# Half-row transposes in pairs, and one double place in PSUM in place of two single ones, in a decoder step's sample attention

## The chip, the cores and the metric

The kernel runs on one core of one Trainium2 chip. The metric is the device time of one execution in microseconds; runs of one kernel are compared by their median. The profile and the trace come from one further, profiled execution. Engines are named as in the profile: PE is TensorE's matrix product, PEld its weight load, DVE is VectorE, ACT is ScalarE, POOL is GpSimd, SP is SyncE. L1513 is line 1513 of the kernel.

## The reference, cut to what matters

One inference step of a two-layer decoder: an mLSTM layer, then a forgetting-attention layer, each followed by a SwiGLU network. Two groups of requests share the weights: a prompt of 1024 tokens, and 8 sample requests of 8 new tokens each with 512 tokens of paged history. The change lies in the attention of the sample requests:

```python
kp = cache_k[page_table].reshape(Bd, n_pages * PAGE_SIZE, H_B, DH_B)     # 8 requests, 4 pages of 128 rows
...
s = jnp.einsum('bqhd,bkhd->bhqk', qi, k, preferred_element_type=f32)     # 16 heads of 64
s = s + ci.astype(f32).transpose(0, 2, 1)[..., None] - ckT[:, :, None, :]
s = jnp.where(pos_k[None, :] <= pi[:, None], s, -jnp.inf)
p = jax.nn.softmax(s, axis=-1)
return jnp.einsum('bhqk,bkhd->bqhd', p.astype(v.dtype), v)
```

## The kernel before

The stage that matters is `attend_sample`, called at the end of `phase_b`. It works request by request (b = 0 to 7) and, in a request, page by page (n = 0 to 3).

- `load(b)` issues the DMA of the request's keys, values and log-forget rows on SP's queue (request 0's small operands go through ScalarE's queue, L1478 to L1491). `kp` holds 4 pages of keys, 128 rows (positions) by 1024 columns (heads and dimensions).
- `turn(b, n)` transposes a page of keys with TensorE: eight transposes of 128 x 128 in 4-byte floats (L1513), each with the page's block as the loaded operand and the identity as the moving one. They go in two groups of four, each group into one PSUM bank (`ktp`, tag "kt"; the pool gives that tag two places of a bank each). VectorE copies the first group to `kT` in SBUF and ScalarE the second (L1514).
- `score(b, n)` multiplies queries with the transposed page, in tiles of 32 columns of the array (L1522). `new_keys(b)` does the same for the new tokens' keys (L1532), adds the forget terms and takes the row maximum on VectorE (L1535, L1537), and calls the exponentials on ScalarE (L1382).
- `turn_p(b)` transposes the request's weights, 128 rows by 576: four whole transposes into a place of tag "kt" (L1547), copied by ScalarE (L1548), and a fifth for the 64 new positions into a spare part of the bank of `new_keys` (L1549), copied by VectorE (L1550).
- `product(b)` multiplies the weights with the pages of values (L1559); `out(b)` transposes the result (L1570) and writes it to `ys`.

TensorE's order is written out by hand. Between these pieces stand calls f(n), each of which issues n times three matmuls of another work, the output gate of the layer: `gates()` in `phase_b` (L62 to L64, tile `bps`, 384 or 336 columns, whole rows of the array). Each gate tile of 24 matmuls ends with a sigmoid on ScalarE (L1328, tile `ogb`) that needs another activation table than the exponentials, so a table load stands between them. Where a weight of the gate is prepared, ScalarE rounds it (L126) and VectorE takes the remainder (L127). A round for the request x = b + 1 reads:

```python
load(x); f(2); turn(x, 0); f(2); turn(x, 1); f(2); turn_p(b); f(3)
score(x, 0); product(b); score(x, 1); f(2); turn(x, 2); f(2); out(b); turn(x, 3)
f(3); score(x, 2); score(x, 3); new_keys(x)
```

The order on the other engines is set by a scheduler when the kernel is built. A place of a tag is written again only after all readers of the tile that held it are done. The next stage, `attend_prompt`, loads its first operands on SP's queue (L1717). Elsewhere in the kernel stand other matmuls on half the array's rows, which the prediction reads: `scores` of the prompt attention (L1751), two heads on rows 0 to 63 and 64 to 127 into two banks, and `chunk_scores` of the mLSTM (L816); and small transposes of 16 rows in `forget` (L1368).

Of the kernel before, what the change touches and what calls it, by code (L numbers as in the profile page):

```python
# [7 lines left out]
F32 = mybir.dt.float32  # L8
# [8 lines left out]
P = 128  # L17
# [3 lines left out]
NS = NB * NQ  # L21
# [14 lines left out]
PAGE, NPG = 128, 4  # L36
PAST = PAGE * NPG
# [1431 lines left out]
def attend_sample(self, sk, sp, s2, pp, cq, ncn, masks, Y, fill):  # L1469


    nc, I, O = self.nc, self.I, self.O
# [3 lines left out]
    kt = sp.tile([P, 8, T0], F32, name="ktS")  # L1476
# [29 lines left out]
    def turn(b, n):  # L1506

        R = rows[b]
        kT = R["kT", n] = early.pop(0) if early else s2.tile([P, 8, PAGE], F32, name=f"kT{b}{n}", tag="kT")
        for g in range(2):  # L1510
            pk = pp.tile([P, 4, P], F32, name=f"ktp{b}{n}{g}", tag="kt")
            for j in range(4):
                nc.tensor.transpose(pk[:, j, :], R["kp"][n][:, (4 * g + j) * P : (4 * g + j + 1) * P], self.ident)  # L1513
            (nc.scalar.copy if g else nc.vector.tensor_copy)(kT[:, 4 * g : 4 * g + 4, :], pk)  # L1514

    def score(b, n):
        R = rows[b]
# [23 lines left out]
    def turn_p(b):  # L1541
        R = rows[b]
        s, pn = R["s"], R["pn"]
        pt = R["pt"] = s2.tile([P, 5, P], F32, name=f"ptS{b}", tag="ptS", bufs=1)
        ps = pp.tile([P, 4, P], F32, name=f"ptp{b}", tag="kt")
        for n in range(NPG):
            nc.tensor.transpose(ps[:, n, :], s[:, n * P : n * P + P], self.ident)  # L1547
        nc.scalar.copy(pt[:, :4, :], ps)  # L1548
        nc.tensor.transpose(pn[:NS, 64 : 64 + P], s[:, PAST:], self.ident)  # L1549
        nc.vector.tensor_copy(pt[:NS, 4, :], pn[:NS, 64 : 64 + P])  # L1550

    def product(b):
        R = rows[b]
# [23 lines left out]
    load(0)  # L1577
    f(3)
    turn(0, 0)
    f(2)  # L1580
    turn(0, 1)
    f(2)
    for n in range(NPG):
        score(0, n)
        f(2)
        if n + 2 < NPG:
            turn(0, n + 2)
            f(2)
    new_keys(0)
    for b in range(NB):  # L1590
        x = b + 1
        if x == NB:
            f(4)
            turn_p(b)
            f(3)
            product(b)
            f(3)
            out(b)
            break
        load(x)  # L1600
        f(2)
        turn(x, 0)
        f(2)
        turn(x, 1)
        f(2)
        turn_p(b)
        f(3)
        score(x, 0)
        product(b)
        score(x, 1)  # L1610
        f(2)
        turn(x, 2)
        f(2)
        out(b)
        turn(x, 3)
        f(3)
        score(x, 2)
        score(x, 3)
        new_keys(x)
# [3 lines left out]
    for g in range(2):  # L1623
# [9 lines left out]
        for j in range(4):  # L1633
            for z in range(2):
                r = slice(z * 64, z * 64 + 64)
                nc.vector.tensor_copy(Q[r, j, (2 * j + z) * NM : (2 * j + z + 1) * NM], qt[r, 4 * g + j, NS:])
        pn = pp.tile([P, 512], F32, name=f"mps{g}", tag="sn", bufs=1)
        for j in range(4):
            nc.tensor.matmul(pn[:, :NM], Q[:, j, :], kt[:, 4 * g + j, NS:], start=(j == 0), stop=(j == 3))
        s = s2.tile([P, NM], F32, name=f"sM{g}", tag="sM")  # L1640
# [6 lines left out]
        pt = s2.tile([NM, P], F32, name=f"ptM{g}", tag="ptM")  # L1647
# [6 lines left out]
        for z in range(2):  # L1654
            r = slice(z * 64, z * 64 + 64)
# [275 lines left out]
```

## Time and profile before

| | |
|---|---|
| three runs, median (lowest to highest) | 3142.53 us (3132.64 to 3145.92) |
| the profiled execution: its time, its span | 3134.74 us, 3133.0 us |
| PE busy; PEld busy | 3034.0 us (97%); 2883.1 us (92%) |
| DVE; ACT; POOL busy | 1265.6 us (40%); 950.2 us (30%); 412.2 us (13%) |
| granted TensorE clock, mean | 0.987 |
| sample attention, transposes at L1513 | 256, from 1716.6 us to 1861.9 us of the span |

Times in the profile are microseconds from the span's start, and means of one instruction are in nanoseconds. A row of the timeline gives start, length, engine, line, operation, output and inputs, the loaded operand's rows x columns and the moving one's shape, and in brackets the engine's idle time before it with what ended it. Matmuls are pipelined, so that the length of one is more than the distance to the next.

### The profile page before, as it was taken

Reading aid. Unit: us, or ns where it says so; the run is one execution under the profiler, and the core shown is the slowest. Engines: PE = TensorE matmul, PEld = TensorE weight load, DVE = VectorE, ACT = ScalarE, POOL = GpSimd, SP = SyncE. Lnnn points to the kernel's source line nnn. Section 1 sums busy time; section 2 is a strip of 40 time slices with the busy share of each in tenths; the row PEclk is TensorE's granted clock in tenths of the full one; section 3 lists DMA queues with packets and bytes.
Section 4 is the critical chain, followed back from the end, with each engine's and each line's share of the span. In section 5 each row is a group of like instructions: output and inputs, shape, how many; then the busy total and the mean of one; then the engine's idle time right before and its main releaser. Section 6 shows DMA issues by size and latency. Waiting matters only on the chain.

```text
span 3133.0 us, 50924 instructions
## 1 busy us (share of the span) xinstructions
PE 3034.0 (97%) x21182; PEld 2883.1 (92%) x21182; DVE 1265.6 (40%) x2678; ACT 950.2 (30%) x1873; POOL 412.2 (13%) x806
## 2 busy tenths in 40 slices
PE   7999989999999999999999998999999999999998
PEld 7998879999999999999999886777999999999998
DVE  5132545633333333272455433554453333333323
ACT  5122453311111111142445445666331111111112
POOL 2011322100000000044453011222210000000002
PEclk9999999999999999999999998999999999999999
DMA  6142544111111111134444854332311111111111
GB/s 212 33 117 82 140 120 123 47 48 41 45 43 41 48 41 48 41 112 141 152 156 126 297 207 167 110 124 75 113 48 41 47 41 43 45 41 48 41 41 58
DMA packets 243314, 277.85 MB, mean 89 GB/s; under 512 B 26510, under 2 KB 193866, under 8 KB 243082
## 3 DMA queue, kind: packets, MB, share of 16 engines
q1 hardware_dynamic: 215426, 195.88, 19.9%
q0 software_dynamic: 23984, 76.40, 7.5%
q8 instruction: 166, 2.72, 0.4%
q10 hardware_dynamic: 3672, 2.31, 0.3%
q14 instruction: 66, 0.54, 0.1%
HBM read 211.35 MB, written 63.18 MB: 88 GB/s over the span
## 4 chain that ended last, share of the span: by engine, by line
PE 79%; DVE 4%; ACT 2%; DMA 2%; issue 1%; POOL 0%; SPq 0%; ACTq 0%; DVEq 0%; POOLq 0%
PE fps L63 11%; PE fps L62 11%; PE fps L64 11%; PE dps L62 5%; PE dps L63 5%; PE dps L64 5%; PE tmps L62 3%; PE tmps L63 3%; PE tmps L64 3%; PE sp L1751 3%; PE tp L1793 2%; PE op L1816 2%; PE pops L64 2%; PE pops L63 2%; PE pops L62 2%
## 5 line engine op out<-in xcount | busy, mean ns | idle before, releaser
L133 DVE TENSOR_TENSOR slot<-slot,slot 128x1024 fp32r<-128x1024 f32 x140 | 171.9, 1229 | 483.7 <-ACT slot L132 483.6
L132 ACT CAST slot<-slot 128x1024 fp32r<-128x1024 f32 x140 | 147.1, 1051 | 707.9 <-PE dps L63 393.7
L62 PE MATMUL dps<-ah,slot 128*128 128x384 f32 (+1 forms) x1056 | 353.1, 334 | 6.1 <-DVE vA L1075 3.1
L63 PE MATMUL dps<-al,slot 128*128 128x384 f32 (+1 forms) x1056 | 349.1, 331 | 0.0
L64 PE MATMUL dps<-ah,slot 128*128 128x384 f32 (+1 forms) x1056 | 348.7, 330 | 0.0
L205 POOL TENSOR_TENSOR ns<-ns,nq 128x384 f32<-128x384 f32 (+1 forms) x72 | 80.9, 1123 | 1717.6 <-ACT nq L203 1717.5
L62 PE MATMUL fps<-x1h,slot 128*128 128x384 f32 x704 | 236.9, 337 | 0.0
L62 PE MATMUL fps<-x2h,slot 128*128 128x384 f32 x704 | 236.5, 336 | 0.0
L63 PE MATMUL fps<-x2l,slot 128*128 128x384 f32 x704 | 236.5, 336 | 0.0
L64 PE MATMUL fps<-x2h,slot 128*128 128x384 f32 x704 | 236.5, 336 | 0.0
L64 PE MATMUL fps<-x1h,slot 128*128 128x384 f32 x704 | 236.5, 336 | 0.0
L63 PE MATMUL fps<-x1l,slot 128*128 128x384 f32 x704 | 236.4, 336 | 0.0
L64 PE MATMUL fps<-x0h,slot 128*128 128x336 f32 x704 | 223.0, 317 | 0.0
L62 PE MATMUL fps<-x0h,slot 128*128 128x336 f32 x704 | 222.5, 316 | 0.0
L63 PE MATMUL fps<-x0l,slot 128*128 128x336 f32 x704 | 222.4, 316 | 0.0
L62 PEld LDWEIGHTS dps<-ah,slot 128*128 128x128 f32 x1056 | 198.3, 188 | 13.9 <-DVE vA L1075 6.6
L63 PEld LDWEIGHTS dps<-al,slot 128*128 128x128 f32 x1056 | 198.5, 188 | 0.2
L64 PEld LDWEIGHTS dps<-ah,slot 128*128 128x128 f32 x1056 | 198.3, 188 | 0.0
L1053 DVE TENSOR_TENSOR fs<-fps,fs 128x336 f32<-128x336 f32 x132 | 71.4, 541 | 282.7 <-PE fps L64 282.7
L1075 DVE TENSOR_TENSOR Ht<-Ht,dps 128x384 f32<-128x384 f32 (+1 forms) x240 | 125.7, 536 | 106.0 <-PE dps L64 106.0
L1075 DVE TENSOR_TENSOR vA<-vA,dps 128x384 f32<-128x384 f32 (+1 forms) x240 | 125.4, 535 | 91.2 <-PE dps L64 91.2
L132 ACT CAST ah<-fs 128x336 fp32r<-128x336 f32 x132 | 65.7, 498 | 282.0 <-DVE fs L1053 282.0
(560 smaller groups left out, 7335.2 us busy)
## 6 DMA issues: line engine op xcount, KB each, us to landing
slot<-in_w_gate_up SPq DMA_DIRECT2D x88, 512.0 KB
slot<-in_w_down SPq DMA_DIRECT2D x44, 512.0 KB
kp<-in_cache_k SPq DMA_DIRECT2D x32, 512.0 KB
vp<-in_cache_v SPq DMA_DIRECT2D x32, 512.0 KB
wraw<-in_w_in_a SPq DMA_DIRECT2D x24, 512.0 KB
ncb<-cD SPq DMA_DIRECT2D x16, 520.0 KB
slot<-in_w_qo_b SPq DMA_DIRECT2D x16, 512.0 KB
slot<-in_w_kvf SPq DMA_DIRECT2D x14, 512.0 KB
```

The lines of the kernel that those rows point to most:

```text
L62: mm(ps, sh, mh, start=first, stop=False)
L63: mm(ps, sh, ml, start=False, stop=False)
L64: mm(ps, sl, mh, start=False, stop=last)
L132: self.nc.scalar.copy(hi, src)
L133: self.nc.vector.tensor_tensor(out=lo, in0=src, in1=hi.bitcast(F32), op=ALU.subtract)
L205: (nc.vector if x == KT - 1 else nc.gpsimd).tensor_tensor(out=s, in0=s, in1=sq, op=ALU.add)
L1053: nc.vector.tensor_tensor(out=s[:, :n], in0=ps[:, :n], in1=s[:, :n], op=ALU.mult)
L1075: nc.vector.tensor_tensor(out=H[t][:, m], in0=H[t][:, m], in1=o, op=ALU.add)
L1751: nc.tensor.matmul(ps[z][:, :n], a[r, qs], b[r, at : at + n], start=(x == 0), stop=(x == 2 and not diag))
L1793: nc.tensor.transpose(pt[:, x, z, u * P : u * P + P], ss[z, u][:, (j0 + x) * P : (j0 + x + 1) * P], self.ident)
L1816: mm(po[ds[z], :256], vr[:, j0 + x, ds[z]], th[:, x, z], start=(j0 + x == 0), stop=False)
```

## The change

In `turn`, a page's block of 128 columns is transposed in two halves, rows 0 to 63 and rows 64 to 127 of the page, each with its part of the identity. All sixteen halves of a page go into one tile of two banks, the first halves into one and the second into the other, the two halves of a block one behind the other in the order. VectorE copies the bank of the first halves, ScalarE that of the second. In `turn_p` the weights are transposed likewise, the new positions with them in the same tile. The tile has the tag "kt" with one place of two banks in place of two places of one bank. In the built program TensorE issues 16 transposes a page in place of 8 and 10 per request for the weights in place of 5. The scheduler's order for ScalarE, VectorE and SP differs from before inside this stage alone; GpSimd's is the same.

```diff
         kT = R["kT", n] = early.pop(0) if early else s2.tile([P, 8, PAGE], F32, name=f"kT{b}{n}", tag="kT")
-        for g in range(2):
-            pk = pp.tile([P, 4, P], F32, name=f"ktp{b}{n}{g}", tag="kt")
-            for j in range(4):
-                nc.tensor.transpose(pk[:, j, :], R["kp"][n][:, (4 * g + j) * P : (4 * g + j + 1) * P], self.ident)
-            (nc.scalar.copy if g else nc.vector.tensor_copy)(kT[:, 4 * g : 4 * g + 4, :], pk)
+        pk = pp.tile([P, 2, 8, 64], F32, name=f"ktp{b}{n}", tag="kt", bufs=1)
+        for j in range(8):
+            for h in range(2):
+                r = slice(h * 64, h * 64 + 64)
+                nc.tensor.transpose(pk[:, h, j], R["kp"][n][r, j * P : j * P + P], self.ident[r, r])
+        for h in range(2):
+            (nc.scalar.copy if h else nc.vector.tensor_copy)(kT[:, :, h * 64 : h * 64 + 64], pk[:, h])
...
         pt = R["pt"] = s2.tile([P, 5, P], F32, name=f"ptS{b}", tag="ptS", bufs=1)
-        ps = pp.tile([P, 4, P], F32, name=f"ptp{b}", tag="kt")
-        for n in range(NPG):
-            nc.tensor.transpose(ps[:, n, :], s[:, n * P : n * P + P], self.ident)
-        nc.scalar.copy(pt[:, :4, :], ps)
-        nc.tensor.transpose(pn[:NS, 64 : 64 + P], s[:, PAST:], self.ident)
-        nc.vector.tensor_copy(pt[:NS, 4, :], pn[:NS, 64 : 64 + P])
+        ps = pp.tile([P, 2, 8, 64], F32, name=f"ptp{b}", tag="kt", bufs=1)
+        for n in range(NPG + 1):
+            m = P if n < NPG else NS
+            for h in range(2):
+                r = slice(h * 64, h * 64 + 64)
+                nc.tensor.transpose(ps[:m, h, n], s[r, n * P : n * P + m], self.ident[r, r])
+        half = lambda x: x.rearrange("p n (h q) -> p h n q", h=2)
+        nc.scalar.copy(half(pt[:, :4]), ps[:, :, :4])
+        nc.vector.tensor_copy(half(pt[:NS, 4:5]), ps[:NS, :, 4:5])
```

## The prediction

> **What bounds the kernel now.** I read the page first, for the engine that carries the chain, then the stage in which the edited lines run, by windows, and inside it the timeline.
>
> ```profile
> span 3133.0 us, 50924 instructions
> ...
> PE 3034.0 (97%) x21182; PEld 2883.1 (92%) x21182; DVE 1265.6 (40%) x2678; ACT 950.2 (30%) x1873; POOL 412.2 (13%) x806
> ...
> PE 79%; DVE 4%; ACT 2%; DMA 2%; issue 1%; POOL 0%; SPq 0%; ACTq 0%; DVEq 0%; POOLq 0%
> ...
> 1716.00:1742.00 26.00, 19.80 (x154) 16.41 (x156) 8.91 (x32) 8.96 (x17) 4.31 (x8) 0.80 0.96 320
> ...
> 1742.00:1868.00 126.00, 124.77 (x1477) 107.95 (x1477) 51.71 (x159) 58.76 (x103) 7.59 (x14) 1.00 0.71 255
> ...
> L1513 PE MATMUL ktp<-ident,kp 128*128 128x128 f32 x256 | 35.2, 279 | 5.4 <-DVE kT L1514 2.7 <-DVE blo L1272 1.4 <-ACT kT L1514 1.2
> ```
>
> TensorE bounds the kernel. The windows show the stage of the sample attention: first 26 us in which TensorE has holes and its clock is at 0.80, then 126 us in which it is busy for 124.77 and everything added to its queue is added to the end. The last row is what the change replaces: 256 whole transposes, eight for each of 32 pages. Nothing after this stage hides a delay: the loads of the next stage wait for one of this stage's last matmuls.
>
> ```profile
> SPq L1717 <- PE pom L1652: 5.4, 1, 5.4
> ```
>
> Now one round of the stage (a request's new pages 0 and 1, then the weights of the request before), out of the timeline with other rows left out. Columns: start in us, length, engine, line, operation.
>
> ```profile
> 1778.56 0.34 PE L64 MATMUL bps<-x1h,slot 128*128 128x384 f32 x1
> ...
> 1778.73 1.03 PE L1513 MATMUL ktp<-ident,kp 128*128 128x128 f32 x8
> ...
> 1779.14 0.78 ACT L1382 ACTIVATE sS<-sS,nb 128x576 f32<-128x576 f32 x1 [2.33 <-DVE nb L1380]
> ...
> 1779.44 0.69 DVE L1514 COPY kT<-ktp 128x512 f32<-128x512 f32 x1 [0.33 <-PE ktp L1513]
> ...
> 1779.78 0.34 PE L63 MATMUL bps<-x1l,slot 128*128 128x384 f32 x1
> ...
> 1779.91 0.57 ACT L1514 COPY kT<-ktp 128x512 f32<-128x512 f32 x1
> ...
> 1779.95 0.34 PE L64 MATMUL bps<-x1h,slot 128*128 128x384 f32 x1
> ...
> 1780.65 1.04 PE L1513 MATMUL ktp<-ident,kp 128*128 128x128 f32 x8
> ...
> 1781.78 0.59 ACT L1514 COPY kT<-ktp 128x512 f32<-128x512 f32 x1 [1.30 <-PE ktp L1513]
> ...
> 1781.88 0.34 PE L64 MATMUL bps<-x1h,slot 128*128 128x384 f32 x1
> ...
> 1782.38 1.28 ACT L1328 ACT_TABLE_LOAD   x1
> ...
> 1782.39 0.34 PE L64 MATMUL bps<-x2h,slot 128*128 128x384 f32 x1
> ...
> 1782.57 0.60 PE L1547 MATMUL ptp<-ident,sS 128*128 128x128 f32 x4
> ...
> 1783.29 0.34 PE L63 MATMUL bps<-x2l,slot 128*128 128x384 f32 x1
> ...
> 1783.68 0.49 ACT L1328 ACTIVATE ogb<-bps 128x384 f32<-128x384 f32 x1
> ...
> 1784.07 0.58 ACT L1548 COPY ptS<-ptp 128x512 f32<-128x512 f32 x1
> ```
>
> The reader is to see that TensorE never stops here, that a gate matmul follows the next at 0.17 (1779.78 to 1779.95), and that the weights' transposes at 1782.57 run while ScalarE is still at the page's second copy (until 1782.37) and has the table load and the gate's sigmoid (ogb) still before it. Before the change they needed only VectorE's place of the pair, which was free.
>
> **What the transposes cost, before and after.** Before, a page takes from L64 at 1778.56 to the second gate matmul at 1779.78, 1.22, less two gate periods of 0.17: 0.88. The weights take 1783.29 - 1782.39 - 0.34 = 0.56. So a whole transpose is 0.11.
>
> Half-row transposes in pairs are not in this trace. Half-row matmuls in pairs are, and so are transposes with few moving columns:
>
> ```profile
> 1909.58 0.34 PE L64 MATMUL og<-x1h,wlo 128*128 128x384 f32 x1
> ...
> 1909.85 0.79 PE L1751 MATMUL sp<-k,q 64*128 64x384 f32 x6
> ...
> 1910.85 0.34 PE L63 MATMUL og<-x1l,whi 128*128 128x384 f32 x1
> ...
> 326.89 1.16 PE L816 MATMUL sps<-qk 64*128 64x128 f32 x16
> ...
> 1457.17 0.66 PE L1368 MATMUL fgcq<-ident,cnB 16*128 16x16 f32 x8 [1.10 <-DVE cnB L1364]
> ...
> L1368 PE MATMUL fgcq<-ident,cnB 16*128 16x16 f32 x8 | 0.7, 210 | 1.1 <-DVE cnB L1364 1.1
> ```
>
> The first three rows price the way into half rows and out again: 1910.85 - 1909.58 = 1.27, less two gate periods and three pairs of the same 0.17 each, leaves 0.41 that whole rows do not pay. L816 shows that two halves run side by side in plain 4-byte data too: 16 passes of 128 columns in 1.16, where one after the other at 0.11 would take 1.76. L1368 gives the beat of transposes that load 128 columns and move few: (0.66 - 0.21) / 7 = 0.064. With 64 moving columns the moving side needs half of 0.11, 0.055, so the load's 0.064 is the later of the two; I take 0.064 for a pair (0.055 to 0.11, the upper end if the two halves take turns). In the 0.41 is a first load that nothing hides; at L1368's beat it should be some 0.05 shorter than in the L1751 rows (an estimate), so I take 0.36 for the way in and out, with 0.41 as the upper end and nothing as the lower (transposes with fewer rows might not pay it).
>
> A page: 0.36 + 8 x 0.064 = 0.87 against 0.88. The weights, five pairs: 0.36 + 0.32 = 0.68 against 0.56. So the 32 pages gain 0.3 together and the eight weights lose 1.0. What halving the rows saves goes into entering and leaving.
>
> The copies move as many elements and I cost them as before (0.69, 0.57). Both now start behind the last pair, VectorE's about 0.1 later and ScalarE's earlier than before. The small loads nm and cm, which the change moves ahead of some of request 1's pages on SP's queue, are short, and no row of TensorE waits for a page; I cost them at nothing (a page that came late would cost its lateness once).
>
> **One place in place of two.** Now a block may begin only when both copies of the block before are done. In the built program the queue of ScalarE for a round reads: exponentials, copy of page 0, table load, sigmoid ogb, copy of page 1, copy of the weights; before, page 1's copy stood ahead of the table load. And ogb waits for a gate matmul that TensorE issues behind page 1's transposes. The round above, by its own rows: page 0 starts at 1778.83 (0.10 of way in, as 1909.85 - 1909.58 - 0.17), its last pair at 1779.34; 0.21 for that pair (L1368's mean) and 0.09 to the copy (1781.69 to 1781.78) make the copies ready at 1779.64, VectorE's done at 1780.33; ScalarE's stays at 1779.91 to 1780.48, because the exponentials of 1779.14 hold it. Six gate matmuls later page 1 would start at 1780.72: no wait. Its last pair starts at 1781.23, the last gate matmul of ogb at 1781.83 and ends at 1782.17. ogb then starts at 1782.20; the copy follows 0.39 behind it (as 1784.07 follows 1783.68), 1782.59 to 1783.18; the weights' transposes start at 1783.23. Unwaited they would start at 1782.62. Behind TensorE's waiting instruction stand nine gate matmuls, the scores and the products, all on the path. The stall is 0.61, and the round's third block ends 0.69 later than before. Pages 2 and 3 have no sigmoid between their copies. So five such rounds: 5 x 0.67 = 3.4.
>
> Two of the seven rounds are worse, since a late exponential holds page 0's copy:
>
> ```profile
> 1763.27 0.56 ACT L1514 COPY kT<-ktp 128x512 f32<-128x512 f32 x1
> 1763.74 0.70 ACT L126 ACTIVATE slot<-slot,gain 128x128 fp32r<-128x128 f32 x2
> ...
> 1763.89 0.66 PE L1513 MATMUL ktp<-ident,kp 128*128 128x128 f32 x4 [0.61 <-ACT kT L1514]
> ...
> 1765.38 0.60 PE L1547 MATMUL ptp<-ident,sS 128*128 128x128 f32 x4
> ```
>
> Here half of page 1 was already done when TensorE waited. After, all of it starts at 1763.89, and on ScalarE one rounding of a weight (0.4, two take 0.70), the table load, ogb and the copy follow: 1763.8 + 0.4 + 1.28 + 0.39 + 0.58, so the weights start near 1766.45, not 1765.38. With the way out of their block 1.1 each (the second such round begins near 1813.5), 2.2.
>
> The start of the stage:
>
> ```profile
> 1722.46 0.66 PE L1513 MATMUL ktp<-ident,kp 128*128 128x128 f32 x4 [1.92 <-DVE kT L1514]
> ...
> 1726.09 0.52 PE L63 MATMUL bps<-x1l,slot 128*128 128x384 f32 x1
> 1726.41 0.52 PE L64 MATMUL bps<-x1h,slot 128*128 128x384 f32 x1
> ...
> 1726.74 0.60 ACTq L1491 DMA_DIRECT2D nck<-csE  x1
> ...
> 1727.38 1.07 ACT L1514 COPY kT<-ktp 128x512 f32<-128x512 f32 x2 [6.22 <-DMA qDh<-bhi]
> ...
> 1728.49 1.11 DVE L1503 COPY qb<-qtS 64x32 f32<-64x32 f32 x8 [4.65 <-DMA qtS<-qS]
> ...
> 1729.00 1.08 PE L1522 MATMUL sps<-kT,qb 128*32 128x128 f32 x16 [2.07 <-DVE qb L1503]
> ```
>
> ScalarE's first copy sits behind its own loads until 1727.38. Before, page 1 and six gate matmuls were done meanwhile and TensorE then idled 2.07 for qb. After, page 1 starts at about 1728.0; page (0.87 to 1.5) and gates (6 x 0.17, or 6 x 0.32 at the low clock of the 1726.09 rows) put the first scores at 1729.9 to 1731.4, not 1729.0: 0.9 to 2.4, I take 1.7 since the clock is low there.
>
> Sum: 3.4 + 2.2 + 1.7 + 0.1 (the last weights; request 0's other pages come out even) = +7.4 us. The profiled execution lasted 3134.7 (its span 3133.0 and 1.7 around it) and would become 3142.1. The median of the three runs, 3142.5, lies 7.8 above that execution; the same addition gives 3149.9.
>
> **Rivals.**
> - The waits do not bind, only the ways in and out: the sum keeps the blocks' 0.7 and 1.7 of the start, 3145. For it: the stall hangs on ogb's place in one queue. Against: the built order has it in all seven rounds. Chance 0.18.
> - The pairs take turns. This is the way to slower: two half-row transposes, moved and loaded one after the other, 0.064 more per pair, (32 x 8 + 8 x 5) x 0.064 = 19 on top of 7.4, 3169. It decides from a beat of about 0.09 for a pair. Against it stands L816; for it, that no row has two transposes at once. Chance 0.09.
> - The loads set a slower beat. If a half-row load of 128 columns takes as long as a whole transpose does, 0.11 instead of 0.064, 296 pairs add 13.6: 3163.5. L1368's beat speaks against it, though its loads have 16 rows. Chance 0.08. (The Trainium skill, TensorE: Matmul & The Clock Gate, section LDWEIGHTS, has this rule: a load lasts its columns divided by 1.2 ns, whatever its rows, which is 107 ns for 128; by it halving rows would save nothing. L1368's 64 ns disagrees with it.)
> - The promise holds: no price for entering half rows and no new wait. A page falls from 0.88 to 0.57, 32 x 0.31 + 8 x 0.18 = 11.4 less, 3131. Against: every half-row block in the trace pays. Chance 0.05.
>
> **How the numbers follow.** The forecast of 3149.9 has 0.60. About 0.5% (15.7 us) is what a measurement of this kernel can tell from no change; its three runs lie 13.3 apart. Slower by more: the two slow-beat rivals, 0.17, and a little of the forecast's own upper edge, 0.19 in all. Faster by more: only the promise with luck in the runs, 0.02. The range leaves out the promise and the turn-taking pairs: from 3136 (the first rival, with runs as far below as those of before lie) to 3164 (the slow loads).
>
> **What would show it.** In the trace of after: a beat of 0.055 to 0.07 in 16 half-row transposes and a page at 0.87; TensorE's idle time before ptp, put down to the ScalarE copy, near 0.6 in five rounds and more in two; about 7.5 us of idle in front of the second page of request 0, and scores starting 1 to 2.4 later; the stage's end 7 later; the rest unchanged. It would be wrong with a beat near 0.11, with ptp unwaited, or with a page well under 0.8.

## The result: 3151.9 us, 0.35% longer

| | before | after |
|---|---|---|
| median (lowest to highest), eight runs each | 3141.36 us (3132.64 to 3146.31) | 3151.91 us (3145.08 to 3158.26) |
| ratio, 95% interval | | 1.0035 (1.0018 to 1.0052) |
| profiled execution: time, span | 3134.74, 3133.0 us | 3153.29, 3151.6 us |
| the stage, in the profiled execution | 150.7 us | 166.9 us |

The forecast of 3149.9 is 2 us off and inside its range; the time stays within the 0.5% that the prediction took for no change. That hides that the sum behind it was too small where it can be checked. **The stage** is measured here, and for every kernel below, from the last gate matmul ahead of the first page's transposes to the last request's weights' transposes: 1716.63 to 1867.28 before, 1719.00 to 1885.89 after. It grew by 16.2, and the prediction's terms gave 7.4. Behind that point both executions are alike (1265.7 us to the end in each), ahead of it they differ by 2.4, as executions of one kernel do.

The page and the windows of the changed kernel:

```profile
span 3151.6 us, 51506 instructions
...
PE 3040.3 (96%) x21478; PEld 2877.6 (91%) x21478; DVE 1267.4 (40%) x2678; ACT 950.2 (30%) x1873; POOL 412.2 (13%) x806
...
PE 79%; DVE 4%; ACT 3%; DMA 2%; issue 2%; POOL 0%; ACTq 0%; SPq 0%; DVEq 0%; POOLq 0%
```

```profile
1716.00:1742.00 26.00, 17.17 (x172) 13.97 (x170) 10.59 (x38) 9.02 (x21) 4.16 (x8) 0.87 0.93 300
1742.00:1868.00 126.00, 113.59 (x1530) 88.83 (x1530) 47.51 (x147) 53.64 (x95) 7.05 (x13) 0.97 0.69 251
```

In the same 126 us TensorE was busy for 124.77 before and is for 113.59 now: the work is no longer the limit, it waits. The groups of TensorE in the stage (busy, mean of one in ns, then the idle time ahead of them and what ended it) say where:

```profile
L1514 PE MATMUL ktp<-ident,kp 64*128 64x64 f32 x512 | 23.5, 234 | 15.4 <-ACT kT L1516 10.3 <-DMA kp<-in_cache_k 2.9 <-DVE blo L1272 1.7
...
L1552 PE MATMUL ptp<-ident,sS 64*128 64x64 f32 x64 | 3.7, 235 | 6.8 <-ACT kT L1516 6.8
```

That is 22.2 of idle time, against 5.4 ahead of the pages' transposes and the 2.07 for qb before: 14.7 more. ScalarE's copy of a page ends 17.1 of the 22.2 (1.2 before). The round that answers to the one shown of before (same request, other rows left out):

```profile
1790.06 0.34 PE L64 MATMUL bps<-x1h,slot 128*128 128x384 f32 x1
...
1790.33 0.71 PE L1514 MATMUL ktp<-ident,kp 64*128 64x64 f32 x16
...
1791.15 0.69 DVE L1516 COPY kT<-ktp 128x512 f32<-128x512 f32 x1 [0.54 <-PE ktp L1514]
1791.25 0.34 PE L63 MATMUL bps<-x1l,slot 128*128 128x384 f32 x1
...
1791.88 0.59 ACT L1516 COPY kT<-ktp 128x512 f32<-128x512 f32 x1 [0.37 <-DVE kT L1516]
1791.95 0.34 PE L64 MATMUL bps<-x1h,slot 128*128 128x384 f32 x1
1792.48 1.28 ACT L1328 ACT_TABLE_LOAD   x1
...
1792.52 0.71 PE L1514 MATMUL ktp<-ident,kp 64*128 64x64 f32 x16 [0.23 <-ACT kT L1516]
...
1793.27 0.69 DVE L1516 COPY kT<-ktp 128x512 f32<-128x512 f32 x1 [1.36 <-PE ktp L1514]
...
1793.98 0.49 ACT L1328 ACTIVATE ogb<-bps 128x384 f32<-128x384 f32 x1 [0.21 <-PE bps L64]
...
1794.13 0.34 PE L64 MATMUL bps<-x2h,slot 128*128 128x384 f32 x1
1794.37 0.58 ACT L1516 COPY kT<-ktp 128x512 f32<-128x512 f32 x1
...
1795.00 0.52 PE L1552 MATMUL ptp<-ident,sS 64*128 64x64 f32 x10 [0.53 <-ACT kT L1516]
```

The reader is to see three things. The block itself is as forecast: 1791.25 - 1790.06 less two gate periods is 0.85, and 0.71 less the mean length of one, 0.23, leaves 0.48 for fifteen steps, 0.032 for a transpose or 0.064 for a pair. The wait behind the sigmoid is as forecast: the weights start at 1795.00, 0.87 behind the gate matmul at 1794.13, where an unwaited block starts 0.27 behind (1790.33 after 1790.06). And one thing was not forecast: ScalarE's copy of page 0 at 1791.88 waits for VectorE's copy of the same page, 1791.15 to 1791.84, and so page 1 has to wait too. Before the change both copies ran together (1779.44 and 1779.91). The list of waits in the stage (us in total, times, the longest) has this as the largest wait of ScalarE; it is idle time of ScalarE, of which only a part reaches TensorE:

```profile
ACT kT L1516 <- DVE kT L1516: 60.9, 18, 8.5
...
PE ktp L1514 <- DMA kp<-in_cache_k: 2.9, 1, 2.9
```

### The profile page after: what moved, and what is told of

It is laid out like the page before. It is cut to its first block, busy times and chain, and to the rows that moved or that the text cites. A ratio compares the mean times of both kernels' runs of the same rounds, so it can differ in the third digit from the quotient of the medians.

```text
span 3151.6 us, 51506 instructions
## 1 busy us (share of the span) xinstructions
PE 3040.3 (96%) x21478; PEld 2877.6 (91%) x21478; DVE 1267.4 (40%) x2678; ACT 950.2 (30%) x1873; POOL 412.2 (13%) x806
## 3 DMA queue, kind: packets, MB, share of 16 engines
q1 hardware_dynamic: 215426, 195.88, 19.9%
## 4 chain that ended last, share of the span: by engine, by line
PE 79%; DVE 4%; ACT 3%; DMA 2%; issue 2%; POOL 0%; ACTq 0%; SPq 0%; DVEq 0%; POOLq 0%
PE fps L63 11%; PE fps L62 11%; PE fps L64 11%; PE dps L62 5%; PE dps L63 5%; PE dps L64 5%; PE tmps L62 3%; PE tmps L63 3%; PE tmps L64 3%; PE sp L1756 3%; PE tp L1798 2%; PE op L1821 2%; PE pops L64 2%; PE pops L63 2%; PE pops L62 2%
```

## Experiments

First a table of the stages; "ratio" is to the kernel before, run on the same chip in the same job.

| kernel | stage, us | ratio (95% interval) |
|---|---|---|
| before | 150.7 | 1 |
| after | 166.9 | 1.0035 (1.0018 to 1.0052) |
| e1, halves of kT unbroken | 165.5 | 1.0044 (1.0027 to 1.0061) |
| e2, whole rows in one place | 169.9 | 1.0083 (1.0064 to 1.0101) |
| e3, half rows, two places | 154.3 | 1.0012 (0.9999 to 1.0026) |
| e4, halves not in pairs | 174.8 | 1.0067 (1.0045 to 1.0089) |
| e5, a tile for each half | 153.1 | 1.0021 (1.0004 to 1.0037) |
| e6, no sigmoid | 160.9 | 1.0046 (1.0031 to 1.0061) |
| e7, four loads for 32 | 169.3 | 1.0050 (1.0031 to 1.0069) |
| e8, two pages at a time; again | 144.0; 143.6 | 0.9987 (0.9970 to 1.0003); 0.9996 (0.9981 to 1.0010) |
| e9, e8 with the small loads | 146.3 | 1.0006 (0.9993 to 1.0019) |

The stage is the sharper measure, since it leaves out what executions of one kernel differ by elsewhere; it comes from one execution each.

**Why the copies follow one another.** The first guess was the interleaved destinations: VectorE's half and ScalarE's half of kT lie in alternating runs of 64.

```diff
-kT = ... s2.tile([P, 8, PAGE], F32, ...)
+kT = ... s2.tile([P, 2, 8, 64], F32, ...)
-    (nc.scalar.copy if h else nc.vector.tensor_copy)(kT[:, :, h * 64 : h * 64 + 64], pk[:, h])
+    (nc.scalar.copy if h else nc.vector.tensor_copy)(kT[:, h], pk[:, h])
```

> The changed kernel, but kT is laid out by halves (half, eight parts, 64 keys), so that each of a page's two copies writes one unbroken half of its tile; the scores read it across the two halves; nothing else differs (every engine's queue has the same order). The stage is measured from the last gate matmul before the first page's transposes to the last request's weights' transposes: 150.7 us before, 166.9 after. Theory 1 (the two copies of a page follow one another in the changed kernel because their destinations interleave in one tile): ScalarE's copy starts beside VectorE's again, the waits before pages 1 and 3 (0.2 to 0.4 each, 14 of them) go, the waits of the weights behind the sigmoid stay near 0.6: the stage lasts 162 to 163. Theory 2 (they follow one another because they read one PSUM tile): no change, 166 to 168.

```profile
ACT kT L1516 <- DVE kT L1516: 60.8, 18, 8.0
```

Theory 1 fell: the wait is the same (60.8 against 60.9), so are the waits before pages 1 and 3, and the stage is 165.5, a little below the range that theory 2 gave. The destination is not what orders the copies.

**One place without half rows.**

```diff
-for g in range(2):
-    pk = pp.tile([P, 4, P], F32, name=f"ktp{b}{n}{g}", tag="kt")
-    for j in range(4):
-        nc.tensor.transpose(pk[:, j, :], R["kp"][n][:, (4 * g + j) * P : (4 * g + j + 1) * P], self.ident)
-    (nc.scalar.copy if g else nc.vector.tensor_copy)(kT[:, 4 * g : 4 * g + 4, :], pk)
+pk = pp.tile([P, 8, P], F32, name=f"ktp{b}{n}", tag="kt", bufs=1)
+for j in range(8):
+    nc.tensor.transpose(pk[:, j, :], R["kp"][n][:, j * P : (j + 1) * P], self.ident)
+for g in range(2):
+    (nc.scalar.copy if g else nc.vector.tensor_copy)(kT[:, 4 * g : 4 * g + 4, :], pk[:, 4 * g : 4 * g + 4, :])
```

> The kernel before with its whole-row transposes, but a page's eight and a request's four of the weights go into one place of two banks with one buffer, as in the change: one place without half rows. Theory 1 (the loss is the one place and what it does to the order on ScalarE): the weights wait near 0.6 in five rounds and about 2 in two, the second page of request 0 waits for ScalarE's first copy, no waits before page 3, and one page of request 2 may come late (up to 3) as in the changed kernel, since SyncE's order is nearly that of the changed kernel: the stage lasts 159 to 162. Rival (the loss is the half rows, in and out of their mode): 151 to 153.

```profile
ACT kT L1514 <- DVE kT L1514: 64.5, 18, 8.2
...
PE ktp L1512 <- ACT kT L1514: 13.9, 15, 7.3
...
PE ptp L1547 <- ACT kT L1514: 6.8, 7, 2.1
```

The rival (half rows cost) fell. But 169.9 is above what theory 1 gave too, since the copies follow one another here as well, with unbroken destinations and whole rows. And with one place whole rows are the worse choice: by the rows of one round in each kernel their eight transposes take 1.03 - 0.28 = 0.75 from the first to the last, not 0.48, and the first copy can begin only then; in five rounds TensorE waits 0.6 to 0.7 before page 1 (0.3 to 0.4 in the changed kernel), and in all seven 0.5 to 0.6 before page 3 (0.2 to 0.3).

**Half rows with two places, and half rows with one place but a tile for each half.** Both give each half its own tile of one bank. e3 leaves the pool two places and the weights whole rows in VectorE's place; e5 has one place per half, for pages and weights, as the change has.

```diff
-pk = pp.tile([P, 2, 8, 64], F32, name=f"ktp{b}{n}", tag="kt", bufs=1)
+pk = [pp.tile([P, 8, 64], F32, name=f"ktp{b}{n}{h}", tag="kt") for h in range(2)]                    # e3
+pk = [pp.tile([P, 8, 64], F32, name=f"ktp{b}{n}{h}", tag=f"kt{h}", bufs=1) for h in range(2)]        # e5
...
+ps = [pp.tile([P, 8, 64], F32, name=f"ptp{b}{h}", tag=f"kt{h}", bufs=1) for h in range(2)]           # e5
```

> The changed kernel's half rows in pairs for the pages alone, each half in a bank of its own with two places as before, kT by halves, and the weights by whole rows into VectorE's place as before: half rows without one place. Theory 1: a page block of 0.85, no wait of the weights behind the sigmoid, ScalarE's order as before; the second page of request 0 still waits for ScalarE's first copy (about 1.5), and a page of request 2 may come late (up to 3), since SyncE's order is that of the changed kernel; the pages gain 32 x 0.035 = 1.1: the stage lasts 151 without a late page, 154 with one. Rival (half rows are what costs): over 158.

> The changed kernel, but each half has a tile and a one-bank place of its own (one buffer each) in place of one two-bank tile, for the pages and for the weights; the destinations interleave as in the change. So there is still only one place per half, but no instruction shares a tile with the other half's copy. In the built program ScalarE's copy of page 1 then stands ahead of the table load and the sigmoid, as in the kernel before. Theory A (the one tile is the cause: ScalarE's copy waits for VectorE's, and the scheduler, which plans with that wait, puts page 1's copy behind the sigmoid): copies side by side, no wait before pages 1 and 3, no wait of the weights behind the sigmoid in five rounds; the start and a late page of request 2 (up to 3) stay: the stage lasts 152 to 156 (166.9 in the change, 150.7 before). Theory B (one place per half is the cause, since a block waits for both copies of the block before): over 160.

e3 came out at 154.3, as expected with a late page. The page came 1.9 late, though, where that figure had counted 3; another 1.5 is a wait of one request's products for VectorE's copy of the weights, which was not expected. e5 is the one that decides, 153.1: theory A. Its round of the same request:

```profile
1781.56 0.69 DVE L1516 COPY kT<-ktp 128x512 f32<-128x512 f32 x1 [1.21 <-PE ktp L1514]
1781.58 0.59 ACT L1516 COPY kT<-ktp 128x512 f32<-128x512 f32 x1 [0.33 <-PE ktp L1514]
...
1783.40 0.69 DVE L1516 COPY kT<-ktp 128x512 f32<-128x512 f32 x1 [1.08 <-PE ktp L1514]
1783.49 0.59 ACT L1516 COPY kT<-ktp 128x512 f32<-128x512 f32 x1 [1.32 <-PE ktp L1514]
1784.10 1.28 ACT L1328 ACT_TABLE_LOAD   x1
1784.55 0.52 PE L1552 MATMUL ptp<-ident,sS 64*128 64x64 f32 x10
```

The copies of one page start 0.02 to 0.09 apart, page 1's copy stands ahead of the table load again, and the weights' row has no bracket: no wait. So one place per half costs little: 2.4 against before, in which are 2.1 at the start of the stage and 1.6 of pages that came late. The rest of the 16.2, 13.8, goes when each half has a tile of its own. Not all of it is the price of the one tile: some 1.3 is pages that came less late than the 2.9 of the changed kernel, and some 2.8 a lower clock in its round of request 2 (worked out below), which e5 does not have (1.00 from 1762.8 to 1780.0). The one *tile* costs twice over: the program makes ScalarE's copy wait for VectorE's where both read one tile, and in the kernels with such a tile and the sigmoid (after, e1, e2, and e4 and e7 below) the scheduler put page 1's copy behind the table load and the sigmoid, in both without (e3, e5) ahead of them.

**How much of the wait of the weights is the sigmoid's.**

```diff
-nc.scalar.activation(s[:, :n], ps[:, :n], AF.Sigmoid)
+nc.vector.tensor_copy(s[:, :n], ps[:, :n])
```

> The changed kernel without the sigmoid of the gates in this stage (ogb): VectorE copies the gate sums instead, so the table loads go too and ScalarE's queue runs from page 1's copy to the weights' copy with nothing between (the gates' values are left out). If the weights wait for the sigmoid, as the prediction has it, the waits of 0.57 in five rounds and most of the 2.2 in two go, 5 to 7 together, while the 0.2 to 0.4 before pages 1 and 3 stay: the stage lasts 158 to 162. If they wait for the chain of copies anyway: 164 to 167.

```profile
ACT kT L1516 <- DVE kT L1516: 73.7, 25, 7.3
...
PEld ptp L1552 <- ACT kT L1516: 4.1, 7, 0.6
```

The stage, 160.9, is in the first range, but the story is mixed. The two long waits of the weights (2.2 each) shrank to 0.4, while in the five rounds 0.3 of 0.6 stayed: there the chain of the two copies is late without a sigmoid. The waits before page 1 grew in four rounds (to 0.8 to 1.05). VectorE's queue has another order there: the reciprocal of the exponentials' sums (L1383), which waits for ScalarE, stands ahead of page 0's copy, and in the changed kernel behind it.

```profile
1782.50 0.16 DVE L1383 RECIPROCAL nb<-nb 128x1 f32<-128x1 f32 x1 [0.94 <-ACT sS L1382]
1782.58 0.67 DVE L1516 COPY kT<-ktp 128x512 f32<-128x512 f32 x1
```

So e6 changes more than the sigmoid, and its split of the wait is rough.

**Do pairs run side by side?**

```diff
-for j in range(8):
-    for h in range(2):
+for h in range(2):
+    for j in range(8):
```

> The changed kernel, but a page's eight transposes of the upper rows come first and the eight of the lower rows behind them, so that neighbours never lie in different row halves; the other engines' queues are the same. If neighbours of a pair run side by side, as I read the changed kernel's 16 starts in 0.49, then 16 come at 0.055 to 0.065 each: first to last 0.85 to 1.0, a page block of 1.25 to 1.35, 32 x 0.45 = 14 more less some of the waits for copies (VectorE's can start earlier): the stage lasts 175 to 181. Rival (a half-row transpose has a beat of 0.03 by itself, and the pairing does nothing): page block 0.85, the stage 165 to 167.

```profile
1790.34 0.34 PE L64 MATMUL bps<-x1h,slot 128*128 128x384 f32 x1
...
1790.61 1.01 PE L1514 MATMUL ktp<-ident,kp 64*128 64x64 f32 x16
...
1791.55 0.45 PE L62 MATMUL bps<-x1h,slot 128*128 128x384 f32 x1
...
1791.84 0.33 PE L63 MATMUL bps<-x1l,slot 128*128 128x384 f32 x1
```

Neighbours on different row halves overlap more than neighbours on the same half: the same sixteen in the other order take 1.01 in place of 0.71, the block 1.16 in place of 0.85. The rival (0.03 whatever the order) fell. Whether a pair gains by its loads or by its moving columns, these rows do not tell. The step is 0.052 ((1.01 - 0.23) / 15), a little below what I had expected, and the stage, 174.8, just under its range.

**The late page.** In the changed kernel request 2's first page comes late. SyncE's queue ahead of it, and the transposes that wait:

```profile
1759.99 0.42 SPq L1633 DMA_DIRECT2D nm<-cD  x1
1760.45 0.42 SPq L1634 DMA_DIRECT2D cm<-cD  x1
1761.11 0.96 SPq L1495 DMA_DIRECT2D vp<-in_cache_v  x2
...
1767.81 0.71 PE L1514 MATMUL ktp<-ident,kp 64*128 64x64 f32 x16 [2.90 <-DMA kp<-in_cache_k]
```

The page's load was issued at 1762.26, behind a row of small loads (19 by SyncE's rows since request 1's last page, not the 27 of the expectation below); in the kernel before at 1751.49.

```diff
-for h in range(8):
-    hh = 8 * g + h
-    nc.sync.dma_start(nm[h * NM : (h + 1) * NM], self.cD[hh, :NM].partition_broadcast(NM))
-    nc.sync.dma_start(cm[h * NM : (h + 1) * NM], self.cD[hh, :NM].unsqueeze(1))
+heads = self.cD[8 * g : 8 * g + 8, :NM]
+nc.sync.dma_start(nm, heads.unsqueeze(1).broadcast_to([8, NM, NM]))
+nc.sync.dma_start(cm, heads.unsqueeze(2))
```

> The changed kernel with the 32 small loads nm and cm (16 partitions each) as four loads of 128 partitions. SyncE issues a small load every 0.46 in the changed kernel's trace, and 27 of them stand between request 1's last page and request 2's first, whose page comes 2.9 late. If those issues are the cause, request 2's pages are issued about 10 earlier and nothing waits for a page: the stage lasts 163 to 164.5. If the page is late for another reason (its buffer, the values ahead of it): 166 to 167.

Half right. No page is late any more (request 2's first block starts 0.27 behind its gate matmul), so the small loads were the cause. But the stage is 169.3, longer, because the scheduler moved what uses them ahead as well: on VectorE's queue the sum on nm now stands in front of VectorE's copy of request 0's third page and waits for its load. TensorE then waits 2.0 before the fourth page, and the clock behind that wait is 0.61 (1739.6 to 1744.0).

```profile
1738.23 0.18 DVE L1634 TENSOR_TENSOR nm<-nm,m 128x16 f32<-128x16 f32 x1 [6.24 <-DMA nm<-cD]
1738.32 0.68 DVE L1516 COPY kT<-ktp 128x512 f32<-128x512 f32 x1
```

**A version made from this.** Half rows pay their way in and out once per block, 0.33, so a block of two pages pays half as often. It takes four one-bank tiles; one bank came from the gates (two for three), one from letting the new keys' scores share the products' place; the weights go by whole rows. The round's calls follow: pages 2 and 3 go together too, and request 0 scores two pages behind each block.

```diff
+pk = [[pp.tile([P, 8, 64], F32, name=f"ktp{b}{m}{h}", tag="kt", bufs=4) for h in range(2)] for m in (n, n + 1)]
+for i in range(2):
+    for j in range(8):
+        for h in range(2):
+            r = slice(h * 64, h * 64 + 64)
+            nc.tensor.transpose(pk[i][h][:, j], R["kp"][n + i][r, j * P : j * P + P], self.ident[r, r])
...
-        turn(x, 0); f(2); turn(x, 1); f(2)
+        turn(x, 0); f(4)
```

> A version meant to beat both: half rows in pairs, two pages at a time in one block (32 half-row transposes, four one-bank tiles), so that the way in and out of half rows is paid once for two pages; a bank comes from the gates (two in place of three) and one from the new keys' scores, which share the products' place; weights by whole rows; the four large loads of nm and cm. By the measured 0.0324 per half-row transpose and 0.33 for the way in and out, two pages take 0.33 + 32 x 0.0324 = 1.37 in place of 2 x 0.88: 16 x 0.39 = 6.2 less than before, the stage 144 to 146. If two banks for the gates, or four copies behind one block, bring waits of their own: 148 or more. If a longer block pays its way in and out again with every page: 150.

```profile
1806.82 0.34 PE L64 MATMUL bps<-x1h,slot 128*128 128x384 f32 x1
1807.09 1.20 PE L1514 MATMUL ktp<-ident,kp 64*128 64x64 f32 x32
...
1808.22 0.44 PE L62 MATMUL bps<-x1h,slot 128*128 128x384 f32 x1
1808.51 0.33 PE L63 MATMUL bps<-x1l,slot 128*128 128x384 f32 x1
```

Two pages take 1808.51 - 1806.82 - 0.34 = 1.35 (1.37 expected), and the stage 144.0, 6.6 less than before. The time could not be told from that of before, so it ran again, beside the same version with the small loads.

> The version with two pages at a time (e8), but with the 32 small loads of before in place of four large ones. If two pages in one block carry the gain, the stage lasts 144 to 146 where no page comes late (up to 3 more where request 2's first page does), and the time is 2 to 7 below that of before. If the four large loads carried it: 149 to 151 and no difference in time.

> The version with two pages at a time (e8) once more, beside the runs of before of this job, since its stage was 6.6 shorter but its median only 2 lower with an interval that holds 1. The stage 144 to 145, the ratio 0.997 to 0.9995.

The stage is 143.6 again, and 146.3 with the small loads, where a page of request 2 comes 1.8 late and a second one, inside its block, 1.9 late: two pages per block carry the gain, not the loads. The times missed what was expected: e9 is 2 above the kernel before, not 2 to 7 below, and the second run of e8 has 0.9996, just above 0.9995. A gain in time is not shown: every interval holds 1, and 6.6 of 3140 is 0.2%, where the intervals are 0.3% wide. The version beats the changed kernel (whose interval, from 1.0018, lies above all three) and is level with the kernel before.

## Why the prediction was right, and where its sum was not

- **Page and weight blocks** (0.87 and 0.68): right, 0.85 and 0.65 (1.00 from gate matmul to gate matmul less two periods, where the weights did not wait). The way in and out is 0.85 - 16 x 0.032 = 0.33, taken as 0.36. The reason given for the beat was wrong, though. I took 0.064 for the load of a pair; e4 has one load per 0.052 with loads of the same 128 columns and 64 rows, and the pairs one per 0.032. So the load is not what sets 0.064; what does stays open. (The Trainium skill, TensorE: Matmul & The Clock Gate, section LDWEIGHTS, gives a load its columns divided by 1.2 ns, whatever its rows; for 128 columns that works out to an estimate of 107 ns. The trace agrees that rows do not matter to the length of one load, which is 138 ns for 64 rows and 140 for 128; but by their records the loads overlap, one per 52 or 32 ns, so as a distance between loads the rule does not hold here.)
- **The copies, "costed as before"**: the step that failed. I had ScalarE's copy "earlier than before"; it begins 0.7 behind VectorE's, since it waits for it (in the round shown 1.82 behind the last gate matmul, before the change 1.35). From it follow the waits that the prediction denied: "no wait" before page 1 was 0.2 to 0.4 in six rounds and 1.15 in one, 3.1 together, less the 1.7 that the kernel before waited inside page 1 in two rounds; "no sigmoid between" pages 2 and 3 was true, and yet 0.2 to 0.3 in each of seven rounds, 1.6.
- **The wait behind the sigmoid**: 0.61 in five rounds, measured 0.56 to 0.60, from the right place in ScalarE's queue. By e6, roughly half of it has a second cause, the copies one behind the other, which I did not have. (The weights' transposes of before, at 1782.57, do not run while ScalarE is at the page's copy, which ended at 1782.37, but under the table load; no term hangs on that.)
- **The two rounds with a late exponential**: mis-sized. From page 0 to the weights they last 2.7 and 2.4 longer than before, not 1.1 (the first of them at a lower clock); the waits of the weights in them are 2.2 each, against 0.6 that the kernel before waited inside page 1. The chain that I added up left out that page 1 itself waits for copies one behind the other.
- **The start of the stage**: right. The first scores came 14.38 behind the gate matmul against 12.37, 2.0 later (1.7, between 0.9 and 2.4). But it belongs to the pairs, which need both banks, more than to the one place: e3, with two places, has 14.54.
- **SyncE's order, "costed at nothing"**: wrong, 2.9 once, as the prediction's bracket allowed, and a lower clock behind it (below). It is not a fixed price: e2, e3 and e5, with small loads just as far ahead, waited 0.3, 1.9 and 1.6 for pages of requests 2 and 3, e4 nothing.
- **The rivals**: waits that do not bind, pairs in turns and slow loads were all refuted by the trace of after; the promise too, by the 0.33.
- **The total**: put together from the two traces, the 16.2 are 2.0 up to the first scores; 1.4 less from there to request 1's first page, where the clock of before was still at 0.50 (1728 to 1732); 1.0 to 1.1 for each of five rounds, together 5.4 (the prediction had 0.67 each); 2.7 for request 5's round; 3.0 for the late page; and 4.6 for request 2's round. Without its waits that last round takes 19.9 where request 5's, which takes as long as it before the change (18.0 each), takes 17.1; so 2.8 of it is the lower clock, which no term had. Against the 16.2 in the one profiled execution stand 10.6 between the medians (5.7 to 16.3 by the interval). That the forecast met the median within 2 us is therefore in part luck: the waits at the start and behind the sigmoid were about right, the order of the copies, the late page and the clock were not in the sum, and the sum is about half of what the stage shows.

## What to carry to other kernels

Count the waits that a tile brings, not only its places: two engines that read halves of one tile may be put in order by the program, and the scheduler's order changed with it here; two tiles of half the size kept the copies side by side, at a stage of 153.1 in place of 166.9. A mode with a fixed way in and out (here 0.33 around work of 0.52) pays in longer blocks: two pages at a time took 1.35 where whole rows take 1.76. When a scheduler owns the order, look at what it moves on the queues that the edit does not name: here small loads delayed a page by 2.9, and with fewer of them another engine waited.

## What the runs showed of the hardware

TensorE slows down behind some waits. After 2.9 us without work in the changed kernel the granted clock (the last figure but two) fell to 0.66:

```profile
1764.00:1767.80 3.80, 0.91 (x6) 0.61 (x5) 1.58 (x11) 2.95 (x5) 0.00 (x0) 1.00 1.00 390
1767.80:1771.00 3.20, 3.19 (x34) 2.69 (x36) 1.46 (x4) 1.25 (x3) 0.00 (x0) 0.66 1.03 416
```

Sixteen transposes that began 2.6 us after the wait took 0.80 from first to last in place of 0.49; in e3 the same stood behind a wait of 1.9 (0.81). It did not follow every wait: behind the wait of 2.2 in request 5's round the clock stayed at 1.00. In e7 the same wait, ended by ScalarE's copy while the DMA engines had little to do (share 0.16), was followed by 3.3 us at 0.51 (1832.7 to 1836.0), so a busy DMA is not the condition; what is stays open. So a wait can cost more than its length. Half-row transposes on alternating row halves come one per 0.032 us, on the same half one per 0.052, whole ones one per 0.107 ((1.03 - 0.28) / 7 in the prediction's row).
